# Issuing the loads of an add-and-GELU kernel from GpSimd instead of SyncE, behind a short first load

## The chip, the cores and the metric

The kernel runs on one core of one Trainium2 chip. Its time is the device time of one execution in microseconds (us). Most executions of one kernel agree within 0.3%, and all runs used below were fast ones, except one single look that is marked. Engines are named as the profile names them: DVE is VectorE, ACT is ScalarE, POOL is GpSimd, SP is SyncE; SPq and ACTq are the sequencers of SyncE and ScalarE, which issue transfers. L152 is line 152 of the kernel.

## The reference

```python
x, y: 1024 x 4096 float32
z = x + y
out = 0.5 * z * (1 + np.tanh(np.sqrt(2 / np.pi) * (z + 0.044715 * z ** 3)))
```

In all, 33.55 MB are read and 16.78 MB written. The arithmetic is an addition and a GELU, which the kernel writes as z times a sigmoid of a cubic in z.

## The kernel before

The 1024 x 4096 numbers lie as 128 partitions of 32,768. Four loads of x (8192 numbers per partition, 4.19 MB, each) go into one big tile, and four loads of y go into two buffers in turn. Compute works in 16 chunks of 2048: an add (GpSimd, but VectorE for the first), a square on ScalarE, a multiply-add on VectorE, a sigmoid on ScalarE, a multiply on VectorE. Three stores of 8, 5 and 3 chunks end the run. All eleven transfers are issued by SyncE and run in the order of their issue in one queue.

```python
    loads = [8192, 8192, 8192, 8192]
    FIRST = 9
    stores = [16384, 10240, 6144]
    ...
    def load_x(i):
        a, b = lr[i]
        nc.sync.dma_start(out=zt[:, a:b], in_=xv[:, a:b])
    ...                       # load_y likewise, into yt[s]
    def store(i):
        a, b = sr[i]
        ins = nc.sync.dma_start(out=ov[:, a:b], in_=zt[:, a:b])
        if i == 0:            # the first store waits for the multiply of chunk FIRST
            tc.add_manual_dep(ins.ins, muls[FIRST].name, ...)
    ...
    sp = []
    for i in range(len(loads)):
        sp += [(load_x, i), (load_y, i)]
    sp += [(store, i) for i in range(len(stores))]
    pool = [(add, c) for c in range(C) if c in by_pool]
    ...
    begin_early(nc, 2)        # SyncE's first two loads go ahead of the start-up barrier
```

## Time and profile before

| | |
|---|---|
| median of 5 runs | 120.42 us (120.22 to 120.84) |
| span of the profiled run | 118.8 us |
| DMA engines busy | 98.8% of the span |
| busiest compute engine | VectorE, 62% |

The prediction below shows most of the profile. Three more lines of the page are needed for the comparison: what the engines moved in each of 40 slices of the span (2.97 us each), and for two kinds of loads the size in KB and the median time from issue to landing.

```profile
GB/s 243 463 386 497 353 530 353 508 375 475 408 419 463 375 508 353 519 364 508 375 430 452 386 497 353 519 541 353 353 596 463 353 353 441 441 441 441 389 406 265
...
z<-in_x_dram SPq DMA_DIRECT2D x4, 4096.0 KB, 31.4
y<-in_y_dram SPq DMA_DIRECT2D x4, 4096.0 KB, 22.2
```

The row swings between 353 and 596 because each packet is booked whole, and the 16 engines work through equal packets almost in step. Neighbouring slices average to about 433. Only the first and the last are really low.

The trace also records every DMA packet with its start, duration, size and queue. A packet here is what one engine moves for one partition's row of a transfer; I call it a row. Several readings below are worked out from these records, which no printed view lists.

### The profile page before, as it was taken

How to read it: one execution, taken by the hardware profiler on the slowest of the kernel's cores; microseconds unless marked ns; L12 is line 12 of the kernel's file. 1: busy time of each engine (PE TensorE's matmuls, PEld its weight loads, DVE VectorE, ACT ScalarE, POOL GpSimd, SP SyncE). 2: the span in 40 equal slices, each digit the busy share in tenths (PEclk: the TensorE clock that was granted, in tenths of full speed). 3: DMA queues.
4: the chain of work that ended last, by engine and by line, in shares of the span. 5: the costliest groups of instructions: out<-in, count | busy, mean ns of one | idle time of the engine just before them, and what ended most of it. 6: DMA issues, size and time to landing. Idle time of an engine off the chain costs nothing.

```text
span 118.8 us, 172 instructions
## 1 busy us (share of the span) xinstructions
DVE 73.7 (62%) x35; ACT 61.0 (51%) x34; POOL 69.6 (59%) x19
## 2 busy tenths in 40 slices
DVE  0000000635799995739999968999994999990000
ACT  5000000063888965197698647888839779810000
POOL 0000000699996099999959999959999990000000
DMA  7989898989999898989899898998899889999996
GB/s 243 463 386 497 353 530 353 508 375 475 408 419 463 375 508 353 519 364 508 375 430 452 386 497 353 519 541 353 353 596 463 353 353 441 441 441 441 389 406 265
DMA packets 1584, 50.33 MB, mean 424 GB/s; under 512 B 176, under 2 KB 176, under 8 KB 176
## 3 DMA queue, kind: packets, MB, share of 16 engines
q1 hardware_dynamic: 1584, 50.33, 98.8%
HBM read 33.55 MB, written 16.78 MB: 424 GB/s over the span
## 4 chain that ended last, share of the span: by engine, by line
DMA 51%; POOL 26%; POOLq 4%; DVE 4%; DVEq 2%; ACT 2%; issue 0%; SPq 0%
DMA y<-in_y_dram 51%; POOL z L152 26%; POOLq L230 4%; DVE w L163 2%; DVEq L230 2%; DVE z L175 2%; ACT w L157 2%; SPq L128 0%; POOLq L152 0%
## 5 line engine op out<-in xcount | busy, mean ns | idle before, releaser
L152 POOL TENSOR_TENSOR z<-z,y 128x2048 f32<-128x2048 f32 x15 | 69.4, 4658 | 28.3 <-DMA y<-in_y_dram 28.3
L157 ACT ACTIVATE w<-z 128x2048 f32<-128x2048 f32 x16 | 30.1, 1882 | 37.7 <-DVE z L152 21.5
L163 DVE SCALAR_TENSOR_TENSOR w<-w,z 128x2048 f32<-128x2048 f32 x16 | 36.7, 2296 | 11.3 <-ACT w L157 11.1
L175 DVE TENSOR_TENSOR z<-w,z 128x2048 f32<-128x2048 f32 (+1 forms) x17 | 35.9, 2155 | 0.0
L168 ACT ACTIVATE w<-w 128x2048 f32<-128x2048 f32 x16 | 29.7, 1855 | 4.4 <-DVE w L163 4.3
L152 DVE TENSOR_TENSOR z<-z,y 128x2048 f32<-128x2048 f32 x1 | 2.3, 2291 | 20.5 <-DMA y<-in_y_dram 20.5
L215 ACT ACT_TABLE_LOAD x1 | 1.3, 1283 | 1.3 <-PEq L247 1.3
L214 DVE MEMSET one<- 128x1 f32 x1 | 0.1, 59 | 1.3 <-PEq L247 1.3
L247 POOL MEMSET const-float32-0.0<- 128x1 f32 x1 | 0.1, 99 | 0.2 <-issue 0.2
L215 ACT ACTIVATE one<-one 128x1 f32<-128x1 f32 x1 | 0.2, 203 | 0.0
L247 POOL MEMSET const-bfloat16-1.0<- 128x1 bf16 x1 | 0.1, 101 | 0.0
L247 POOL MEMSET const-uint8-127<- 128x1 uint8 x1 | 0.1, 101 | 0.0
L247 POOL MEMSET const-float32-1.0<- 128x1 f32 x1 | 0.1, 98 | 0.0
## 6 DMA issues: line engine op xcount, KB each, us to landing
z<-in_x_dram SPq DMA_DIRECT2D x4, 4096.0 KB, 31.4
y<-in_y_dram SPq DMA_DIRECT2D x4, 4096.0 KB, 22.2
out_dram<-z SPq DMA_DIRECT2D x1, 5120.0 KB, 15.8
out_dram<-z SPq DMA_DIRECT2D x1, 3072.0 KB, 11.9
out_dram<-z SPq DMA_DIRECT2D x1, 22.0
```

The costliest lines, as they stand in the source:

```text
L152: eng.tensor_add(out=zt[:, a:b], in0=zt[:, a:b], in1=yt[s][:, o : o + b - a])
L157: nc.scalar.activation(out=wt[c], in_=zt[:, a:b], func=act.Square, scale=root)
L163: nc.vector.scalar_tensor_tensor(out=wt[c], in0=wt[c], scalar=c1, in1=zt[:, a:b], op0=alu.add, op1=alu.mult)
L168: nc.scalar.activation(out=wt[c], in_=wt[c], func=act.Sigmoid)
L175: ins = nc.vector.tensor_mul(out=zt[:, a + o : a + o + n], in0=wt[c][:, o : o + n], in1=zt[:, a + o : a + o + n],)
L214: nc.vector.memset(one, 0.0)
L215: nc.scalar.activation(out=one, in_=one, func=act.Sigmoid)
L230: tc.compile()
L247: nc = _bacc.Bacc("TRN2", target_bir_lowering=False, num_devices=1)
```

## The change

The intent: SyncE keeps only a short first load of x (2048 numbers per partition, 1 MiB), which bridges the time until GpSimd is ready, and the three stores. GpSimd issues the other loads, each marked as one packet per DMA engine, so that a store in the other queue should not get in between.

```diff
+    HEAD = 2048
+    loads_x = [HEAD, 8192 - HEAD, 8192, 8192, 8192]
     loads = [8192, 8192, 8192, 8192]
 ...
     def load_x(i):
-        a, b = lr[i]
-        nc.sync.dma_start(out=zt[:, a:b], in_=xv[:, a:b])
+        a, b = xr[i]
+        if i == 0:
+            nc.sync.dma_start(out=zt[:, a:b], in_=xv[:, a:b])
+        else:
+            nc.gpsimd.dma_start(out=zt[:, a:b], in_=xv[:, a:b], single_packet=True)
 ...                          # load_y: from sync to gpsimd, single_packet=True
-    sp = []
-    for i in range(len(loads)):
-        sp += [(load_x, i), (load_y, i)]
-    sp += [(store, i) for i in range(len(stores))]
-    pool = [(add, c) for c in range(C) if c in by_pool]
+    sp = [(load_x, 0)] + [(store, i) for i in range(len(stores))]
+    pool = [(load_x, 1), (load_y, 0), (load_x, 2), (load_y, 1), (load_x, 3)]
+    for c in range(C):
+        pool += [(add, c)] if c in by_pool else []
+        if c == 3:
+            pool += [(load_y, 2), (load_x, 4)]
+        if c == 7:
+            pool += [(load_y, 3)]
 ...
-    begin_early(nc, 2)
+    begin_early(nc, 1)
```

More of the change, by code (lines that the diff above doesn't have):

```diff
@@ L108, in ranges @@
         return [(e - f, e) for e, f in zip(ends, sizes)]
-    lr, sr, cr = ranges(loads), ranges(stores), ranges([CH] * (TOT // CH))
+    xr, lr, sr = ranges(loads_x), ranges(loads), ranges(stores)
+    cr = ranges([CH] * (TOT // CH))
     C = len(cr)
@@ L134, in load_y @@
             yt[s] = pool_y.tile([P, YS], fp32, tag="y", name=f"y{s}")
-        nc.sync.dma_start(out=yt[s][:, o : o + b - a], in_=yv[:, a:b])
+        nc.gpsimd.dma_start(
+            out=yt[s][:, o : o + b - a], in_=yv[:, a:b], single_packet=True
+        )
     def store(i):
@@ L202 @@
         ],
-        add: lambda c: [(f, i) for i in over(lr, *cr[c]) for f in (load_x, load_y)],
+        add: lambda c: [(load_x, i) for i in over(xr, *cr[c])]
+        + [(load_y, i) for i in over(lr, *cr[c])],
         sq: lambda c: [(add, c)] + ([(mul, c - PS)] if c >= PS else []),
```

## The prediction

> **What bounds the kernel now.** I read the page of the kernel before first, its slice rows and its table of DMA queues.
>
> ```profile
> span 118.8 us, 172 instructions
> ...
> DVE 73.7 (62%) x35; ACT 61.0 (51%) x34; POOL 69.6 (59%) x19
> ...
> DMA  7989898989999898989899898998899889999996
> ...
> q1 hardware_dynamic: 1584, 50.33, 98.8%
> HBM read 33.55 MB, written 16.78 MB: 424 GB/s over the span
> ```
>
> No compute engine is busy for more than 62% of the span, while the single DMA queue, SyncE's, holds all 16 DMA engines for 98.8% of it. The DMA row is low only in its first slice and its last. So the transfers bind, and only two things can shorten the run: a higher rate while they run, or less lost at the two ends.
>
> The second view is the table of stretches, cut where the loads and stores change (the columns are busy times of VectorE, ScalarE and GpSimd, the clock, the DMA share and the GB/s).
>
> ```profile
> 1.30:21.90 20.60, 0.06 (x1) 1.44 (x2) 0.00 (x0) 1.00 0.95 409
> 37.50:59.30 21.80, 17.89 (x9) 14.88 (x8) 17.95 (x5) 1.00 1.00 433
> 59.30:77.40 18.10, 16.43 (x9) 14.07 (x8) 16.60 (x5) 1.00 1.01 434
> 104.60:118.80 14.20, 2.23 (x2) 0.00 (x0) 0.00 (x0) 1.00 0.93 400
> ```
>
> The middle runs at 433 to 434 GB/s with a share of 1.00. The first stretch loses 5% of 20.6 us, 1.0 us, and the last 7% of 14.2 us, 1.0 us. At 434 GB/s all 50.33 MB would take 116.0 us, and the span is 118.8: 2.8 us is all that lies between this kernel and its own best rate, and most of it is the latency of the first byte and of the last.
>
> The third view is the timeline of SyncE, whose queue carries everything (start, duration; the three stores are one merged line), with the waits of GpSimd beside it.
>
> ```profile
> 0.00 0.38 SPq L128 DMA_DIRECT2D z<-in_x_dram  x1
> ...
> 0.43 0.42 SPq L135 DMA_DIRECT2D y<-in_y_dram  x1
> 1.26 0.33 SPq L128 DMA_DIRECT2D z<-in_x_dram  x1
> ...
> 37.55 0.33 SPq L135 DMA_DIRECT2D y<-in_y_dram  x1
> 37.92 0.43 SPq L128 DMA_DIRECT2D z<-in_x_dram  x1
> 59.33 0.33 SPq L135 DMA_DIRECT2D y<-in_y_dram  x1
> 77.40 29.80 SPq L139 DMA_DIRECT2D out_dram<-z  x3
> ```
>
> ```profile
> 21.94 15.58 POOL L152 TENSOR_TENSOR z<-z,y 128x2048 f32<-128x2048 f32 x3 [21.51 <-DMA y<-in_y_dram]
> ...
> 41.37 17.93 POOL L152 TENSOR_TENSOR z<-z,y 128x2048 f32<-128x2048 f32 x4 [3.85 <-DMA y<-in_y_dram]
> ...
> 60.80 17.95 POOL L152 TENSOR_TENSOR z<-z,y 128x2048 f32<-128x2048 f32 x4 [1.50 <-DMA y<-in_y_dram]
> ...
> 80.25 17.95 POOL L152 TENSOR_TENSOR z<-z,y 128x2048 f32<-128x2048 f32 x4 [1.49 <-DMA y<-in_y_dram]
> ```
>
> Two things are to be seen. Each load is issued well before the queue reaches it: at 37.55 us the fourth load is still running (GpSimd's next adds wait for it until 41.37) and the fifth, 4.19 MB or 9.7 us at 433 GB/s, is behind it, so the queue holds some 13 us of work. And each group of GpSimd's adds begins with a wait for a load: whatever GpSimd does just before, up to 3.85, 1.50 and 1.49 us of it, costs nothing. The chain of waits ends in compute (GpSimd's adds, then the last multiply at 104.64), but that is only the chain of the last store's release. The last store is issued at 106.86, and the trace's records of DMA packets have the store ahead of it running until 110.6 to 111.1. The middle store is issued at 95.75, and the first runs until 98.5 to 99.0. So compute has about 3 us of slack ahead of each.
>
> The packet records give the size of the one term that the change can touch. A packet of 32,768 bytes takes 1213 ns on its engine, one of 65,536 takes 2418, one of 24,576 takes 912. The differences give 27.2 bytes per ns and engine (32,768 bytes in 1205 ns), so about 8 ns of every packet is not data. Sixteen engines at 27.2 make 435 GB/s.
>
> **What the Trainium skill says.** "DMA: Bandwidth & Descriptors", section "Where 436 GB/s comes from", puts the ceiling at 16 ports of 32 bytes at 850 MHz, 435.2 GB/s, for the transfers of all issuers together. The trace agrees: its slope is that number and its steady stretches are at 433 to 434. The same page, section "Queues, rings and completion order", says that an engine takes turns between its queues a whole packet at a time; this kernel has one queue, so nothing of before shows it. The same page, section "Latency and other measured facts", gives a first byte after about 0.6 us from SyncE and about 1 us from GpSimd, and says that engines 7 and 15 tend to be slower where GpSimd writes descriptors. Of the first, the trace shows SyncE's side: issue done at 0.38, first data packet at 1.01, so 0.63 us. The rest it cannot show. "SBUF — State Buffer", section "Who interferes with whom", says that a VectorE instruction with two SBUF inputs keeps GpSimd's reads out. The trace agrees: the first add on GpSimd took 6623 ns against 4500 for the least, while VectorE's only two-input SBUF add ran for 2291. VectorE's other instructions here take one input from PSUM, so they should not hold back GpSimd while it writes descriptors.
>
> **The change part by part.** The bytes, the number of big transfers, the adds, activations and multiplies stay as they are; the order of instructions on VectorE and ScalarE is unchanged.
>
> (a) Packets. Seven loads on GpSimd, each of 8 rows per engine, become one packet per engine instead of eight. If the 8 ns belong to packets, this saves 7 x 7 x 8 ns = 0.4 us per engine. If they belong to rows, it saves nothing. The loads now complete 9.68 us apart (packet records), and the pure data would take 9.64, so seven loads cannot give more than 0.3 us. I take -0.3 us.
>
> (b) The start. SyncE's first load shrinks from 32 KB to 8 KB per partition, 1 MiB, and only it is moved ahead of the start-up barrier. Data begin at 1.0 us as before; the first packets took about 0.57 us longer than later ones, and 1 MiB at 433 GB/s is 2.4 us, so it covers until about 4.0 us. GpSimd is let go at about 1.3. With the skill's 1 us and an issue like SyncE's 0.4, its first data come at about 2.7 us, before the short load is through. So no gap, with 1.3 us in hand. I book +0.2 us as the mean of a gap that may come, since the time that GpSimd takes to issue is not in this trace.
>
> (c) Issue time on GpSimd. Five loads before its first add, which waits until 21.94 anyway; two between its third and fourth chunks of adds (ahead of a wait of 3.85), one before the next group (ahead of 1.50). At up to 1.5 us each they fit into those waits. Even at twice that, the delay ends at the next load's landing. 0 us.
>
> (d) Two queues. The first store is issued at about 77.4, when the last load, landing at 79.7, has about 2.3 us left. In one queue it stands behind. In two, it must take turns, but that load is then in the middle of its single packet on every engine, so it lands first, as before. 0 us. SyncE issues its three stores on the same multiplies as before.
>
> Sum: 120.35 - 0.3 + 0.2, about 120.2 us.
>
> **The rivals.** First, GpSimd's issue is slow at the start: a first-use cost of several us. For it: the trace has no DMA issued by GpSimd. A first byte at 7 us instead of 2.7 would leave the engines idle for 3 us: 123.3 us, slower by over 2%. Second, the loads run slower from GpSimd's rings, on one or two engines at least. Every add waits for all sixteen, so the slowest sets the pace; 2% on 68 us of loads (7 of 9.7 us) is 1.4 us: 121.6; 5% is 3.4: 123.6. For it speaks only the skill's remark. Third, packets do not protect the last load: engines take turns per row of 32 KB, so the two rows left each let a row of the store (64 KB, 2418 ns) go first. The last load lands up to 4.8 us later, the adds behind it too, and the middle store, issued at 95.75 now, comes after the first one's end at 99.0; 1 to 3 us of idle engines, 121 to 123. Against it speaks the purpose of the single packet. Fourth, a rate above the present: the slope of the packets is already the ceiling, and the whole 2.8 us would have to go for a gain of over 2% (2.4 us). I see no way.
>
> **Range and chances.** The mechanism allows at best -0.4 us plus noise, so the low end is 119.5. The high end, 122.0, holds a small gap at the start or a rate lower by 2%. Faster by over 2% needs below 117.9, under the floor given by the ceiling and the latencies: 0.03. Slower by over 2% needs above 122.8, which only the first three rivals in their stronger forms reach: 0.12. Within 2%: 0.85.
>
> **What would show it.** The DMA row of the changed kernel should stay at 8 to 9 after its first slice, with the middle stretches at 433 to 436 GB/s (a); a dip within the first two slices is the first rival; a lower rate all through the loads, with later first adds than 21.9 us, the second; GpSimd's last group of adds starting much later than 80.3 us, the third. Adds that no longer begin with a wait for a load would make (c) wrong. A rate well over 435 GB/s would make the whole argument wrong.

## The result, and the profile after

The changed kernel took 121.88 us (median of 5 runs, 121.26 to 122.12) against 120.42. The ratio is 1.011, with a 95% interval of 1.0078 to 1.0142. Ratios here and below are the mean time of one kernel's runs over that of the other's runs of the same rounds, so they are not quite the ratio of the medians. The kernel got slower by 1.1%, clear of noise and inside the range.

The page of the changed kernel, answering to the lines of before:

```profile
span 119.6 us, 174 instructions
...
DVE 73.7 (62%) x35; ACT 61.0 (51%) x34; POOL 74.0 (62%) x27
...
DMA  6999999999999998989899999998899889999896
GB/s 200 447 411 477 395 482 395 460 416 449 427 416 449 416 460 384 482 384 493 373 460 416 427 449 416 460 526 351 351 460 592 351 351 438 438 438 438 362 427 263
...
q0 software_dynamic: 1152, 32.51, 63.3%
q1 hardware_dynamic: 576, 17.83, 35.4%
```

There are now two queues, 32.5 MB in GpSimd's and 17.8 MB in SyncE's. The DMA row reads 9 where it read 8 and 9 in turn, and nothing in it looks like a gap: the shares of the two queues add up to 98.7%, as before. That is the trap of this profile. A packet counts as busy from its start to its end, also when it takes longer than its size asks for (the slow rows below), so a slow start does not show as idle time. The swing of the GB/s row says more: it has become smaller (395 to 482 early on, where it was 353 to 530), so the engines no longer work in step.

The same stretches as in the prediction, for the changed kernel:

```profile
1.30:21.90 20.60, 0.00 (x0) 0.96 (x2) 2.77 (x5) 1.00 1.00 425
37.50:59.30 21.80, 17.82 (x9) 14.88 (x8) 18.97 (x7) 1.00 1.01 433
59.30:77.40 18.10, 16.45 (x9) 13.54 (x9) 17.18 (x6) 1.00 1.00 427
104.60:118.80 14.20, 2.75 (x2) 0.26 (x1) 0.00 (x0) 1.00 0.94 406
```

The middle runs at 433 as before; nothing was gained there. (The first figure, 425 against 409, cannot be a gain, since the adds at its end start later; short stretches depend on which packets are booked in them.)

And the timeline: SyncE's issues, GpSimd's issues, which are now counted as busy time, and GpSimd's four groups of adds with the wait ahead of each in brackets (PEq L242 is read here as the start-up barrier).

```profile
0.00 0.38 SPq L132 DMA_DIRECT2D z<-in_x_dram  x1
...
1.30 0.69 POOL L134 DMA_DIRECT2D z<-in_x_dram  x1 [0.86 <-PEq L242]
1.99 0.53 POOL L141 DMA_DIRECT2D y<-in_y_dram  x1
...
22.49 15.50 POOL L160 TENSOR_TENSOR z<-z,y 128x2048 f32<-128x2048 f32 x3 [18.41 <-DMA y<-in_y_dram]
...
41.91 17.94 POOL L160 TENSOR_TENSOR z<-z,y 128x2048 f32<-128x2048 f32 x4 [2.53 <-DMA y<-in_y_dram]
...
61.34 17.94 POOL L160 TENSOR_TENSOR z<-z,y 128x2048 f32<-128x2048 f32 x4 [0.62 <-DMA y<-in_y_dram]
...
77.93 29.78 SPq L147 DMA_DIRECT2D out_dram<-z  x3
...
80.76 17.96 POOL L160 TENSOR_TENSOR z<-z,y 128x2048 f32<-128x2048 f32 x4 [1.48 <-DMA y<-in_y_dram]
```

The first adds start at 22.49 where they started at 21.94, the fourth group at 80.76 where it was 80.25: 0.5 us is lost before 22 us and stays lost. Every group still waits for a load, so GpSimd's issuing (0.53 to 0.69 us each) is hidden, as predicted.

The packet records tell where the loss arises. For a row I take its size at 27.2 bytes per ns plus 8 ns as its due time, and call what goes beyond it lost; idle gaps are added, and the sum is averaged over the 16 engines. The last two columns are the times at which the first and the last of the 16 engines finish.

```
kernel          lost in 3-12 us   lost in first      last load       all data
                                  rows of store 1    landed          done
before               0.00 us          0.01 us      79.14 - 79.66   117.83 - 118.34
changed              0.28             0.46         79.45 - 80.26   118.46 - 119.16
```

Two places, then. GpSimd's first rows, just after the short load has ended (its last bytes land at 4.03 to 4.38 us), are slow: at worst 1521 ns instead of 912. This hits the engines unequally, so they drift apart, from 0.5 to 0.8 us between first and last. And at 79.4 to 79.8 us, where the engines pass from the last load to the first store, nine of the sixteen take 3.1 to 3.5 us for a first row that takes 2.42 on the other seven. Measured on the slowest engine, by which the run ends, 0.60 us are there when the last load lands, and another 0.22 come with the store: 0.82, the whole difference of the two profiled spans. (This profiled run, 121.26 us, is the fastest of the five; the next profile below has more of both.)

### The profile page after: what moved, and what is told of

Same layout as the page of the kernel before. It is cut to its first block, busy times and chain, and to the rows that moved or that the text cites. A ratio compares the mean times of both kernels' runs of the same rounds, so it can differ in the third digit from the quotient of the medians.

```text
span 119.6 us, 174 instructions
## 1 busy us (share of the span) xinstructions
DVE 73.7 (62%) x35; ACT 61.0 (51%) x34; POOL 74.0 (62%) x27
## 4 chain that ended last, share of the span: by engine, by line
DMA 50%; POOL 28%; POOLq 4%; DVE 4%; DVEq 2%; ACT 2%; issue 1%; PEldq 0%
DMA y<-in_y_dram 50%; POOL z L160 26%; POOLq L242 4%; DVE w L171 2%; DVEq L242 2%; DVE z L183 2%; ACT w L165 2%; POOL z L134 1%; POOL y L141 0%; POOLq L160 0%; PEldq L242 0%
## 5 line engine op out<-in xcount | busy, mean ns | idle before, releaser
L134 POOL DMA_DIRECT2D z<-in_x_dram x4 | 2.3, 568 | 0.9 <-PEq L242 0.9
L141 POOL DMA_DIRECT2D y<-in_y_dram x4 | 2.2, 550 | 0.6 <-POOL z L160 0.6
```

The costliest lines, as they stand in the source:

```text
L134: nc.gpsimd.dma_start(out=zt[:, a:b], in_=xv[:, a:b], single_packet=True)
L141: nc.gpsimd.dma_start(out=yt[s][:, o : o + b - a], in_=yv[:, a:b], single_packet=True)
```

## The experiments

The theory that I began with: each passage from one queue to another costs some tenths of a us. The rivals: GpSimd's loads are slower all along; or GpSimd's first descriptors merely come too late for so short a first load. Twelve kernels ran besides the result itself, the changed one once more among them. The times first; what they mean follows kernel by kernel. Losses are as defined above, each from one profiled run. The sets ran on three chips, each beside the kernel before, so it is the ratios that can be compared. (One of the twelve, long_head_rows, had a single look; it is told in the last section and is not in the table.)

```
kernel            first load   loads by   median us   ratio (95%)              lost 3-12 us   lost at store 1
changed           1 MiB        GpSimd      121.88    1.0110 (1.0078-1.0142)       0.28          0.46
after_again       1 MiB        GpSimd      121.79    1.0117 (1.0097-1.0137)       0.67          0.79
rows_as_packets   1 MiB        GpSimd      121.84    1.0124 (1.0089-1.0159)       0.71          0.67
head_1024         0.5 MiB      GpSimd      122.31    1.0165 (1.0126-1.0205)       1.03          0.69
head_3072         1.5 MiB      GpSimd      120.30    1.0000 (0.9985-1.0016)       0.00          0.01
head_3072_rows    1.5 MiB      GpSimd      120.46    1.0000 (0.9973-1.0027)       0.00          0.01
head_4096         2 MiB        GpSimd      120.56    1.0002 (0.9982-1.0023)       0.01          0.01
long_head         4 MiB        GpSimd      120.35    0.9997 (0.9985-1.0009)       0.00          0.01
act_early         1 MiB        ScalarE     120.42    0.9997 (0.9983-1.0012)       0.00          0.01
short_head_sp     1 MiB        SyncE       120.72    1.0020 (1.0008-1.0032)       0.00          0.01
pool_early        1 MiB        GpSimd      124.99    1.0361 (1.0324-1.0398)       0.41          0.00
early_store       1 MiB        GpSimd      121.82    1.0102 (1.0081-1.0123)       0.34          0.00
```

### The changed kernel once more

No edit.

> The changed kernel once more, unaltered, as the control of this set. Theory (handovers): where the engines pass from one queue to the other, the first packet of the new queue is slow, as the first of the whole kernel is. In the first profile that was about 0.3 us averaged over the engines at the passage from SyncE's short load to GpSimd's loads (4 to 8 us) and about 0.46 us at the passage from the last load to the first store (79.4 us), nine of sixteen packets 0.7 to 1.0 us too long. Expected: the same two places again, ratio 1.008 to 1.014. Rival (a lower rate of GpSimd's loads all along): rows of 32 KB longer than 1213 ns at the median, and no step at the two passages.

Both places again, and larger: fourteen of sixteen first rows of the store are slow. The ratio is 1.0117, and the median row of 32 KB takes 1213 ns, so a lower rate all along is out. On the slowest engine the last load lands 1.20 us later than in the kernel before (80.86 against 79.66), and the data end 1.59 us later (119.93 against 118.34). Runs of the changed kernel scatter from 121.26 to 122.33 us, and it is the size of the loss at the start that differs between the two profiles.

### Without the single packet

```diff
-            nc.gpsimd.dma_start(out=zt[:, a:b], in_=xv[:, a:b], single_packet=True)
+            nc.gpsimd.dma_start(out=zt[:, a:b], in_=xv[:, a:b])
```

(The same in the loads of y.)

> The changed kernel without the single packet, so that GpSimd's loads are cut into packets in the usual way. If the single packet is what keeps the first store behind the last load, then the last load's landing moves from 80.3 us to as much as 85 and GpSimd's last group of adds from 80.8 to as much as 85.5, the middle store from 96.3 to as much as 101 with idle engines before it: ratio to the kernel before 1.02 to 1.04. If packets make no difference to the turns, the landing stays at 80.3 and the ratio at 1.011. The rows of 32 KB stay at 1213 ns if the 8 ns belong to rows, and become longer than in the single packet if they belong to packets.

The landing of the last load stayed (80.82 us on the slowest engine), the ratio too. So the flag changes nothing visible here, and the rows take 1213 ns with it and without it: the 8 ns belong to rows, not to packets. So it is not the flag that kept the store behind the load here. What an earlier store does is seen below.

### A first load of 4 MiB

```diff
-    loads_x = [HEAD, 8192 - HEAD, 8192, 8192, 8192]
+    loads_x = [8192, 8192, 8192, 8192]
```

(GpSimd's list loses its first load.)

> SyncE loads the whole first quarter of x (4 MiB), GpSimd starts with y. GpSimd is then ready some 8 us before it is needed. Handover theory: the passage costs as much as before, about 0.3 us, now at 10 to 12 us, and the ratio stays at 1.008 to 1.014. Rival (GpSimd's first descriptors come too late for the short load): the cost at the start vanishes, data in the first 25 us run as in the kernel before, and the ratio falls to about 1.006. Because the two queues now both hold work from about 3 us on, the engines may also take turns between rows of x and the whole packet of y; then x lands late with y, and the first adds stay at 22 us.

The whole loss is gone, at the start and at the store, although the engines still pass from SyncE's queue to GpSimd's and from there to the stores. So a passage as such costs nothing, and my first theory falls. Nor was only the part at the start mended, as the rival expected (1.006): the loss at the store vanished with it. It depends on the first loss.

How, the packet records of this and the other profiles show. The first store is released by a multiply, which hangs on an add, which waits for the slowest engine's share of a load. The fast engines are then further ahead of the store's issue. In the changed kernel and in the kernels after_again, rows_as_packets and head_1024, 44 engines finished their last load less than 1.70 us after the issue of the store began; on all 44 the first row of the store was slow, by 0.3 to 1.2 us. Above 1.80 us none was, in these or in the kernels before, head_3072 and long_head; of the engines between, some were. In the kernel before the earliest engine finishes 1.74 us after the issue (79.14 against 77.40), so it just made it. The multiply that releases the store is tuned to the edge.

The records also show the two queues side by side. From 5.3 us on, every engine takes one row of SyncE's and one of GpSimd's in turn, although GpSimd's load is marked as a single packet:

```
one engine, rows of 32 KB with their start in us (H = SyncE's queue, S = GpSimd's)
H 0.99  H 2.73  H 3.97  H 5.18  S 6.39  H 7.60  S 8.81  H 10.02  S 11.23  H 12.44  S 13.65
```

### The short first load by SyncE alone

```diff
+    HEAD = 2048
+    loads_x = [HEAD, 8192 - HEAD, 8192, 8192, 8192]
     loads = [8192, 8192, 8192, 8192]
 ...                          # all loads stay on nc.sync, in the old order
```

> The kernel before with only the first x load cut into 1 MiB and 3 MiB, all on SyncE. Handover theory: no passage between queues, so the time is that of the kernel before within 0.2%, first adds at 21.9 us. Rival (the short load itself, with its 8 KB rows, is what costs at the start): ratio 1.003 or more, and slow packets after the short load as in the changed kernel.

The ratio is 1.002 (1.0008 to 1.0032): a small loss may be real, but no row after the short load is slow and the first adds start at 21.93 us. The short load is not the cause.

### Other lengths of the first load

```diff
-    HEAD = 2048
+    HEAD = 1024      # and 3072, and 4096
```

> A first load of 512 KiB, enough until about 2.9 us. Late first data: the engines stand idle or in slow rows for about 1.2 us more than with 1 MiB; all landings move by that; ratio 1.018 to 1.026, median near 123.2 us. Rival (a passage costs of itself, however long the load ahead of it): ratio 1.012 as with 1 MiB.

> The changed kernel with a first load of 1.5 MiB, which keeps the engines busy until about 5.3 us, 1.3 us longer than with 1 MiB. Theory as before: excess of the first GpSimd rows below 0.1 us, ratio 1.000 to 1.003, between the 1.011 of 1 MiB and the 1.000 of 2 MiB. Rival (the size of the first load matters in proportion): ratio about 1.005 to 1.007.

> The changed kernel with a first load of 2 MiB in place of 1 MiB. Theory now (late first data from GpSimd): GpSimd's issue starts at 1.30 us and its rows flow well only some 3 us later; 1 MiB keeps the engines busy until about 4.0 to 4.4 us, too little by up to 0.9 us on some engines; 2 MiB keeps them until about 6.4. So no slow first rows, the engines stay within 0.5 us of each other, the first store is ready in time, and the ratio to the kernel before is 1.000 (0.998 to 1.002), as with 4 MiB. Rival (a passage between queues costs of itself): ratio still about 1.008 to 1.014.

This is the dose and the response: 1.0165, 1.011, 1.0000, 1.0002. Between 1 and 1.5 MiB the loss disappears altogether; a loss in proportion to the size would have left about half. (That step is clear of noise. The one from 1 to 0.5 MiB is not, by the times alone: the interval of 0.5 MiB, 1.0126 to 1.0205, overlaps with those of 1 MiB and with what I had expected. There the profiles below have to speak.) The views of the profile show it too. For the kernel with 0.5 MiB, the stretch from 4 to 8 us and then, from its timeline, the first adds on GpSimd:

```profile
4.00:8.00 4.00, 0.00 (x0) 0.00 (x0) 0.06 (x1) 1.00 0.89 373
```

```profile
23.43 15.56 POOL L160 TENSOR_TENSOR z<-z,y 128x2048 f32<-128x2048 f32 x3 [19.37 <-DMA y<-in_y_dram]
```

The same two views of the kernel with 1.5 MiB:

```profile
4.00:8.00 4.00, 0.00 (x0) 0.00 (x0) 0.08 (x1) 1.00 1.05 448
```

```profile
21.95 15.51 POOL L160 TENSOR_TENSOR z<-z,y 128x2048 f32<-128x2048 f32 x3 [17.87 <-DMA y<-in_y_dram]
```

With 0.5 MiB a share of 0.89 and 373 GB/s: here the gap is long enough to be seen as idle time, and the adds come 1.5 us later. With 1.5 MiB they start when they did in the kernel before. The miss: 0.5 MiB cost less than I expected (1.0165 against 1.018 to 1.026), probably because with 1 MiB the rows are slow too, without a gap.

The kernel with 0.5 MiB also measures GpSimd's latency. Its issue starts at 1.28 us, the short load's last bytes land at 2.77 to 3.18, and the first GpSimd rows, counted back from their ends by their due time, would have started at 3.7 to 4.5 us, at the median 3.9: 2.6 us after the issue began. In the prediction I had 1.4.

### GpSimd's first two loads ahead of the start-up barrier

```diff
+    early = [i for i in body if i.engine == POOL and isinstance(i, mybir.InstDMACopy)][:2]
+    ...      # moved behind GpSimd's start-up memsets, ahead of the barrier
```

> The changed kernel with its 1 MiB first load, but GpSimd's first two loads are issued ahead of the start-up barrier, at about 0.4 us in place of 1.30. Late first data: GpSimd's rows are then there at about 3.4 us, before the short load is through at 4.0, so the slow rows at 4 to 8 us vanish or shrink below 0.1 us, the engines stay together, and the ratio falls to 1.000 to 1.003. Rival (a passage between queues, or the short load's size, costs of itself): ratio stays at 1.008 to 1.014.

This failed as an experiment on the total, 1.036, for a reason of its own. GpSimd's issues:

```profile
0.86 0.69 POOL L141 DMA_DIRECT2D z<-in_x_dram  x1 [0.42 <-issue]
1.55 0.53 POOL L148 DMA_DIRECT2D y<-in_y_dram  x1
...
23.60 0.53 POOL L141 DMA_DIRECT2D z<-in_x_dram  x1 [21.52 <-PEq L249]
```

Its third load came only at 23.60 us, after a wait of 21.52 at the barrier, which ended 1.1 us after its second load had landed (22.50). That the barrier waits for GpSimd's own transfers is inferred from this. The engines ran dry meanwhile. What can be read is the start: the first issue came at 0.86 us, only 0.4 earlier and not 0.9, and the rows from 3.9 us on were still slow (0.41 us lost). So my expectation of less than 0.1 was missed: from the start of the issue to the end of the short load there were now some 3.0 to 3.6 us, and that is still too little. On ten or more engines the first row came at once and took its due 912 ns, and on most of these a second or third row was slow. So the first byte is not the whole of it: the rows behind it can be late too. That GpSimd is still issuing its other loads meanwhile (until 4.08 us in the changed kernel) is not needed for it, since here it had stopped at 2.08. With 1.5 MiB, where GpSimd's rows ran at full pace from 5.19 us, it was 3.9.

### The loads by ScalarE's hardware queue

```diff
-            nc.gpsimd.dma_start(out=zt[:, a:b], in_=xv[:, a:b], single_packet=True)
+            nc.scalar.dma_start(out=zt[:, a:b], in_=xv[:, a:b])
```

(The same for y; ScalarE issues five loads ahead of its table load, the others after the squares of chunks 3 and 7.)

> The changed kernel with the same 1 MiB first load on SyncE, but the other loads issued by ScalarE's hardware queue in place of GpSimd's, from about 0.8 us on. A hardware queue's first data come 1.0 us after its issue starts, so the second queue's rows are there at about 1.8 us, 2 us before the short load ends. Theory (the second queue must be ready well before the first runs dry; GpSimd is too late for 1 MiB): no slow rows at 4 to 8 us, landings within 0.5 us of each other, ratio 0.998 to 1.003. Rival (two queues or a 1 MiB head cost of themselves): ratio 1.008 to 1.014. If the ratio is raised only at the end, it is the store's turns.

The ratio is 0.9997, with the same 1 MiB and two queues. The first line is ScalarE's first issue in the timeline, the second the stretch from 4 to 8 us:

```profile
0.78 0.38 ACTq L134 DMA_DIRECT2D z<-in_x_dram  x1
```

```profile
4.00:8.00 4.00, 0.00 (x0) 0.89 (x2) 0.00 (x0) 1.00 1.14 489
```

ScalarE began to issue at 0.78 us, 3.4 to 3.8 us before the short load's end (4.16 to 4.53), about the lead that GpSimd had when it issued ahead of the barrier (3.0 to 3.6), and no row was slow. So neither two queues nor the 1 MiB are at fault, but the time that a load takes from GpSimd's issue until its rows run at full pace.

### The first store earlier

```diff
-    FIRST = 9
+    FIRST = 8
```

> The changed kernel with the first store released one multiply earlier, at about 75.7 to 76.4 us in place of 77.9 to 78.6. Two things are open. (1) The slow first packets of the store: if they come from a store issued less than about 1.8 us before an engine runs out of loads, they vanish here. (2) Turns: with the long head the engines took turns row by row between the two queues although GpSimd's load was marked as a single packet. If that holds here, rows of the store (2418 ns each) go between the last load's rows from about 77.6 us on, the last load lands 2 to 5 us later (82.5 to 85 in place of 80.3 to 80.9), GpSimd's last adds start as much later, the middle store comes after the first one's end, and the ratio is 1.015 to 1.035. If the single packet holds the store back, the landing stays and the ratio is 1.007 to 1.010.

The first open point was settled, the second came out as neither of the two forecasts. From the timeline, the stores (merged into one line) and the last adds on GpSimd:

```profile
75.90 34.58 SPq L147 DMA_DIRECT2D out_dram<-z  x3
...
83.55 17.94 POOL L160 TENSOR_TENSOR z<-z,y 128x2048 f32<-128x2048 f32 x4 [4.08 <-DMA y<-in_y_dram]
```

No first row of the store was slow any more (0.00 us): issued 2 us earlier, it was ready in time. But the last two rows of the load were slow instead, by 0.32 us per engine on average (up to 1640 ns in place of 1213).

And the load counted as landed much later. Its last record on each engine is one of 4 bytes, and the load's semaphore, the counter that the adds wait for, counts up 0.3 to 0.4 us after it. In the changed kernel this mark follows the last row at once, at 79.4 to 80.3 us. Here one row of the store got ahead of it on 15 of the 16 engines. One of them:

```
one engine, start in us (S = row of the last load, O = row of the store, M = the load's mark)
S 76.61  S 77.83  S 79.39  O 80.61  M 83.02  O 83.03
```

No row of the store ran between the rows of the load on any engine: the load's data were through at 79.74 to 80.61 us, and the first row of the store began at 79.74. The marks came at up to 83.03 us, 2.8 us later than in the changed kernel, and the wait of GpSimd's last adds grew from 1.48 to 4.08 us. The middle store was issued at 99.05, just as the first one ended (99.07 to 99.94), and the engines stood idle for 0.51 us on average between 98 and 100 us. Gain and loss about cancel, so the ratio is 1.0102 and not 1.015 or more.

So the flag did not keep the store from delaying the load's landing. Whether it kept the store's rows from between those of the load is not shown, as no early store ran without the flag. In the changed kernel the store is late enough to be behind the mark, with the flag and without it.

### The flag by itself, where nothing else is slow

```diff
-            nc.gpsimd.dma_start(out=zt[:, a:b], in_=xv[:, a:b], single_packet=True)
+            nc.gpsimd.dma_start(out=zt[:, a:b], in_=xv[:, a:b])      # with HEAD = 3072; and with the 4 MiB head
```

> The 1.5 MiB head, which has no cost at the start, without the single-packet flag: the term (a) of the prediction by itself. If the flag saved the 8 ns of each row, this kernel would be 0.3 us slower than the one with the flag (ratio to the kernel before 1.0025 against 1.0000). The rows of the two profiles so far were 1213 ns with and without the flag, so the theory expects the same time within 0.1%: ratio 0.999 to 1.001.

> The 4 MiB head without the single-packet flag. With the flag the engines took turns row by row between SyncE's x and GpSimd's y from 5.3 us to about 17 us. If the flag has no effect on the turns here, the sequence of rows and the landing of x (17.3 to 18.9 us) are the same; if it has, the turns have another length (several rows of one queue in a row) and x lands earlier or later by 1 us or more.

With 1.5 MiB the ratio is 1.0000 without the flag and 1.0000 with it: the flag is worth nothing that these runs can tell. (The interval without it, 0.9973 to 1.0027, would by itself still allow the 0.3 us. The rows decide: 1213 ns in both profiles.) The 4 MiB head without it had a single look, state unknown (121.04 us). Its rows alternate one by one just as with the flag; x landed at 17.4 to 17.7 us, where it was 17.3 to 18.9. Why that one run was slow (many rows between 28 and 60 us took 60 to 130 ns too long) stays open, and nothing is built on it.

No experiment beat the kernel before by more than noise. With 1.5 MiB or more, or with ScalarE's queue, it is merely reached again, as a kernel that is at the ceiling of its DMA engines for the whole of its middle must.

## Why the prediction was right, and where it was not

The range and the class held, since the argument for a floor held: the transfers bind, the middle is at the engines' ceiling, and nothing in the change could speed them up. That the median fell inside the range was in part luck: it lies 0.12 us below the upper end of 122.0, and two of the five runs lie above it. The sum of 120.2 us was 1.7 us too low, and three of its steps were off.

(a) Packets: predicted -0.3 us, measured no gain: a row of 32 KB takes 1213 ns with the flag and without it, so the 8 ns belong to rows. The prediction had named that alternative and then chosen the other.

(b) The start: the step that failed in size. It said that GpSimd's "first data come at about 2.7 us" with "1.3 us in hand". With the engines idle they came at the median at 3.9 us, and rows at full pace without any loss were seen only with an issue 3.9 us ahead or more. The +0.2 us booked for it had to be 0.5 to 1.2 us on the slowest engine when the first load of y landed (21.97 and 22.65 us in two profiles, against 21.44).

(c) GpSimd's issue time: right. Seven issues of 0.5 to 0.7 us hid in waits; the smallest wait left was 0.62 us.

(d) Two queues: right that the last load is not held up, wrong in its reason and in its 0 us. The single packet was not what kept the store behind: the load landed as early without it. With the 4 MiB head the engines took turns row by row, marked or not, as the third rival had it; in the changed kernel the store came too late to make use of that. (With the store 2 us earlier the rival's delay came in part, 2.8 us, but by one row of the store ahead of the load's mark.) And the store came too late for the fast engines: 0.22 and 0.39 us more on the slowest path (0.82 - 0.60, 1.59 - 1.20). This follow-up, in which unequal engines at the start turn into a late store at 79 us, was in none of the rivals. For the profiled run of 121.26 us the account closes: 120.35, with 0 for (a), 0.6 for (b) and 0.22 for (d), makes 121.2.

The first rival, a slow start on GpSimd, was the true one, in a weaker form (2.6 us from issue to first data, where the rival had almost 6). The signs that I had laid down to tell it from the second did not work: no dip in the DMA row showed, since a waiting packet counts as busy, and the later first adds, which I had given to a lower rate, came from the start.

## What to carry to other kernels

A load that bridges another engine's start-up must last until that engine's rows run at full pace, not until its first byte is due; sweep its length and take the first value past the step, here between 1 and 1.5 MiB. When the engines bind, look at the spread of their landings and not only at their busy share: a slow start on some engines delays everything that waits for the last of them, and a store tuned to be just in time then comes late for the others. Issuing it earlier is no cure by itself: a load counts as landed only with its last mark, and one row of the store can get ahead of that.

## What the Trainium skill lacked or had wrong

- "DMA: Bandwidth & Descriptors", section "Latency and other measured facts": about 1 us to the first byte from GpSimd. Here the first rows flowed 2.6 us after the issue began (1.9 us after the 0.69 us of the issue), and an issue 3.9 us ahead of need was seen to cost nothing, while with 3.0 to 3.6 us the first row was on time on ten or more engines and on most of these a row behind it was slow. Its 0.6 us for SyncE agrees (0.63). It also says that engines 7 and 15 are usually slower with GpSimd's loads; with a 4 MiB head the last of those loads landed within 0.43 us over the 16 engines (79.10 to 79.53), no wider than SyncE's in the kernel before (0.52), though the engines were not identified one by one.
- The same page, section "Queues, rings and completion order": engines take turns at whole packets, with some nine to 17 descriptors as typical. With the 4 MiB head the turn between SyncE's and GpSimd's queue was a single row of 32 KB (which the profile records as one packet), whether the load was marked as a single packet or not. With the early store one row of the store got ahead of the marked load's last 4 bytes on 15 of 16 engines.
- No page that I read has the lead that a store in another queue needs: below 1.70 us from the start of its issue to the end of an engine's last load, the first row lost 0.3 to 1.2 us on 44 of 44 engines; above 1.80 on none. With the early store, at 3.8 us and more, the load's last two rows were slow instead, by 0.32 us on average.
- No page that I read says that GpSimd's loads issued ahead of the start-up barrier hold up that barrier, as is inferred here from a wait of 21.52 us that ended 1.1 us after they had landed.
